# Tokens for the experts of a mixture-of-experts layer: indirect DMA and transposes in place of one-hot products

## The chip, the cores and the metric

The kernel runs on one core of one Trainium2 chip. The time is the device time of one launch in microseconds. A launch computes one layer of a decoder on 512 tokens: four mixers, then a mixture of experts. A core has a matrix engine (TensorE, PE in the profile; its weight loads stand apart as PEld), three engines for elementwise work (VectorE or DVE, ScalarE or ACT, GpSimd or POOL), SyncE (SP), whose instruction stream here only issues transfers, and 16 DMA engines that move the data. TensorE multiplies a stationary tile, loaded first, with a moving tile; its results go to PSUM banks.

## The reference

Only the second half bears on the change. Each of the 512 tokens (1024 columns) is normalized, the router takes the best 4 of 32 experts for it, and each expert is a gated two-layer network. The results are weighted with the gates and added to the token.

```python
h = rms_norm(x, norm2_g) * (1 + sc2) + sh2
logits = h @ router_w + router_b
top_vals, top_idx = lax.top_k(logits, 4)
gates = softmax(top_vals)
for e in range(32):                      # for the tokens that chose e
    hu = h[tokens] @ w_up[e] + b_up[e]   # 1024 -> 2048
    g, lin = min(hu[:, :1024], 7), clip(hu[:, 1024:], -7, 7)
    y = ((lin + 1) * g * sigmoid(1.702 * g)) @ w_down[e] + b_down[e]
    x[tokens] += gate2 * gates * y
```

All is float32. There are 2048 pairs of token and expert, 64 for an expert in the mean. The weights of the 32 experts are 12 MB each.

## The kernel before

**Two stages.** `emit_pre` (up to about 415 us) computes the modulation, the mixers, the output projection and the routing. The end of it routes the tokens in four tiles of 128: `route(tt)` normalizes a tile `a`, finds its experts, and `place` gives each token a position in each expert's list (`posm`). `emit_moe` (from 415 us on) runs the experts.

**Whole experts and pairs.** The experts are ranked by the number of their tokens. The 16 fullest are run one by one by `whole()`, with up to 128 slots for tokens each. In them each float32 factor is split into a rounded high part and the low rest, and three products replace one: high by high, high by low, low by high. So an expert's 24 weight tiles (8 for each half `hf` of the up projection, 8 for the down projection) are split too: ScalarE makes the high part (`high`, L1475), VectorE subtracts for the low one (`low`, L1480), and a step of six products follows on TensorE (L1610 to L1612 up, L1630 to L1632 down). The other 16 experts are run by `pairs()` two at a time, 64 slots each, in plain float32 products (L1678), each of the two on half of the columns of the array; no weights are split there.

**Order of the work.** `whole()` and `pairs()` are generators; the class `Tasks` takes pieces from both in turn by what each piece is worth (`PACE` is a step of a pair in units of a whole step), so a pair runs among steps of whole experts. TensorE, VectorE and ScalarE execute strictly in the order in which the program is written. The instructions of GpSimd and SyncE are put in order by the framework, and each engine then goes through its own list in that order.

**Weights.** Each weight tile of 1 MB comes by one DMA that SyncE issues (L1460 for the first expert, L1464 for the others) into a first-in-first-out list `fifo` of `RAW` = 8 buffers. A load waits until what read its buffer before is done: VectorE's split for a whole expert, TensorE's product for a pair.

**Tokens.** Before the experts run, all normalized tokens lie in SBUF as a high part `h2H` (ScalarE, L1207) and a low part `h2L` (VectorE, L1208). `select` writes a one-hot matrix (L252): column s of it has a one at the token that fills slot s. `gather_mm` (L261) multiplies `h2H` and `h2L` with it, so that the transposed tokens of two experts (or pairs) come out: 4 x 16 products with 256 columns in an event. `gather_end` (ScalarE, L269) scales and shifts them, and `gather_split` splits them. `slots` (L1490) multiplies the same one-hot matrix with a small table and gives each slot's gate and token number; it ran late in the expert, since only the end needs it. There are 8 such events in `whole()` and 4 in `pairs()`. The tokens of the first expert are built by `first()` while the tiles are routed.

**Bias and results.** A pair's up projection begins with its bias: a product (L1528) with a column `sc` that VectorE copies right before (L1701). An expert ends in `finish`: VectorE scales the result (L1522), and `add_rows` (L1502) adds it to the tokens in memory by an indirect DMA that GpSimd issues, 16 for the whole experts and 16 for the halves of the 8 pairs.

## Time and profile before

| | |
|---|---|
| time, median of 3 runs | 1570.74 us (1563.13 to 1571.32) |
| the profiled execution | 1570.13 us, span 1568.4 us |
| mean granted clock of TensorE | 0.956 of full speed |
| busy: TensorE | 1455.1 us, 93% of the span |
| busy: VectorE | 1018.1 us, 65% |
| busy: ScalarE | 720.2 us, 46% |
| busy: GpSimd | 231.0 us, 15% |
| moved by DMA | 469.54 MB, mean 299 GB/s |

The span is the time from the first to the last instruction that the profiler recorded; the execution's own time is a little longer. A busy share says how much of the span an engine was at work, not that it sets the end.

### The profile page before, as it was taken

The page shows a single profiled execution, that of the slowest core. Times are in us where ns is not written, and L with a number is a line of the kernel's source. Part 1 is how long each engine was busy: PE and PEld are TensorE (multiplying, and loading weights), DVE is VectorE, ACT ScalarE, POOL GpSimd, SP SyncE. Part 2 cuts the span into 40 slices and gives each one's busy share as a digit, 9 for nine tenths or more (in the row PEclk, how much of TensorE's full clock was granted, in tenths as well). Part 3 has the DMA queues.
Part 4 walks back from the last instruction along what each step waited for, and adds up shares of the span by engine and source line. Part 5 has one row for each costly group of instructions (what it writes and reads, how often), then busy time and mean ns, then how long its engine had stood idle before and what let it go on. Part 6 is the DMA issues. An engine that isn't in the chain of part 4 may idle for free.

```text
span 1568.4 us, 19785 instructions
## 1 busy us (share of the span) xinstructions
PE 1455.1 (93%) x6924; PEld 945.9 (60%) x6925; DVE 1018.1 (65%) x1607; ACT 720.2 (46%) x1036; POOL 231.0 (15%) x147
## 2 busy tenths in 40 slices
PE   6898998998979999999999999999999999899995
PEld 5676565666856565565655666565566656556553
DVE  7799776765765674666566565656666575666563
ACT  5463444653534454354544435444454444444441
POOL 3414154533310000000000000010010000001001
PEclk9998997999779999999999999999999999999998
DMA  8362432222647999889899988998999899799994
GB/s 346 111 228 95 135 121 68 88 84 88 235 176 297 375 407 397 306 342 404 347 385 420 403 345 313 393 367 350 421 400 371 331 387 407 308 406 399 398 396 124
DMA packets 73521, 469.54 MB, mean 299 GB/s; under 512 B 8532, under 2 KB 8932, under 8 KB 23240
## 3 DMA queue, kind: packets, MB, share of 16 engines
q1 hardware_dynamic: 70216, 457.21, 73.3%
q0 software_dynamic: 3200, 11.01, 3.7%
q8 instruction: 56, 0.92, 0.2%
q14 instruction: 49, 0.40, 0.1%
HBM read 454.55 MB, written 13.63 MB: 299 GB/s over the span
## 4 chain that ended last, share of the span: by engine, by line
issue 45%; DMA 12%; POOL 1%; POOLq 0%; DVE 0%
DMA out<-af,ii 12%; POOL out L1502 1%; POOLq L1502 0%; DVE af L1522 0%; DVE sc L1701 0%; POOLq L1806 0%
## 5 line engine op out<-in xcount | busy, mean ns | idle before, releaser
L1475 ACT CAST xr<-af 128x1024 fp32r<-128x1024 f32 x288 | 301.9, 1050 | 343.9 <-PE ps_w L1612 229.2
L1678 PE MATMUL ps_p<-af,xg 128*64 128x512 f32 x1536 | 364.1, 610 | 3.0 <-DMA af<-wexp 2.9
L1480 DVE TENSOR_TENSOR ar<-af,xr 128x1024 fp32r<-128x1024 f32 x192 | 235.6, 1230 | 121.3 <-PE ps_w L1611 55.6
L1678 PEld LDWEIGHTS ps_p<-af,xg 128*64 128x64 f32 x1536 | 109.8, 139 | 201.8 <-issue 190.9
L1502 POOL DMA_INDIRECT out<-af,ii x32 | 60.6, 1894 | 1058.5 <-DVE af L1522 919.2
L1610 PE MATMUL ps_w<-xr,ar 128*128 128x512 f32 x384 | 157.1, 409 | 0.0
L1480 DVE TENSOR_TENSOR xr<-af,xr 128x1024 fp32r<-128x1024 f32 x96 | 118.0, 1229 | 60.0 <-PE ps_w L1611 28.6
L1475 ACT CAST ar<-af 128x1024 fp32r<-128x1024 f32 x96 | 100.6, 1048 | 113.5 <-PE ps_w L1612 77.0
L1612 PE MATMUL ps_w<-xr,ar 128*128 128x512 f32 x384 | 151.5, 394 | 0.0
L1611 PE MATMUL ps_w<-ar,ar 128*128 128x512 f32 x320 | 126.7, 396 | 2.4 <-DVE ar L1480 2.4
L261 PEld LDWEIGHTS ps_m<-ar,xb 128*128 128x128 f32 x768 | 97.3, 191 | 18.2 <-issue 8.9
L1480 DVE TENSOR_TENSOR ar<-af,ar 128x1024 fp32r<-128x1024 f32 x64 | 78.2, 1221 | 44.4 <-issue 27.7
L261 PE MATMUL ps_m<-ar,xb 128*128 128x256 f32 (+1 forms) x768 | 100.9, 285 | 4.5 <-DVE ar L252 4.5
L1610 PEld LDWEIGHTS ps_w<-xr,ar 128*128 128x128 f32 x384 | 72.1, 188 | 40.3 <-issue 26.6
L1612 PEld LDWEIGHTS ps_w<-xr,ar 128*128 128x128 f32 x384 | 72.2, 188 | 16.9
L1630 PE MATMUL ps_w<-xr,ar 128*128 128x512 f32 x192 | 80.9, 421 | 0.0
L1611 PE MATMUL ps_w<-xr,ar 128*128 128x512 f32 x192 | 77.0, 401 | 1.2 <-DVE xr L1480 1.2
L1507 ACT ACTIVATE sb<-gb 128x512 f32<-128x512 f32 x48 | 30.4, 633 | 102.9 <-DVE gb L1506 102.9
L1631 PE MATMUL ps_w<-ar 128*128 128x512 f32 x192 | 76.4, 398 | 0.3 <-DVE ar L1480 0.2
L1632 PE MATMUL ps_w<-xr,ar 128*128 128x512 f32 x192 | 76.2, 397 | 0.0
L1611 PEld LDWEIGHTS ps_w<-ar,ar 128*128 128x128 f32 x320 | 60.4, 189 | 15.3 <-DVE ar L1480 4.4
L276 DVE TENSOR_TENSOR ar<-af,ar 128x512 fp32r<-128x512 f32 (+1 forms) x34 | 21.9, 645 | 58.7 <-ACT ar L275 58.5
(444 smaller groups left out, 2479.6 us busy)
## 6 DMA issues: line engine op xcount, KB each, us to landing
af<-wexp SPq DMA_DIRECT2D x384, 1024.0 KB, 9.4
af<-ada SPq DMA_DIRECT2D x32, 512.0 KB, 3.9
xa<-ada SPq DMA_DIRECT2D x4, 1024.0 KB, 11.3
af<-ada SPq DMA_DIRECT2D x4, 1024.0 KB, 15.5
xf<-wout SPq DMA_DIRECT2D x8, 512.0 KB, 3.7
xg<-wout SPq DMA_DIRECT2D x8, 512.0 KB, 3.6
out<-af SPq DMA_DIRECT2D x5, 512.0 KB, 3.0
af<-wG SPq DMA_DIRECT2D x6, 384.0 KB, 9.6
```

Of the source, the lines that this page charges most:

```text
L261: T.matmul(p[:, kk * 256:kk * 256 + n], h[:, tt, k * 128:(k + 1) * 128], Pm[:, tt, 0:n], start=kk == 0 and tt == 0 and h is h2H, stop=kk = ...
L1475: A.copy(wH[i % NH], w)
L1480: V.tensor_tensor(wL[i % NL], ahead.pop(0), wH[i % NH].bitcast(F32), op=OP.subtract)
L1502: G.indirect_dma_start(out=O, out_offset=bass.IndirectOffsetOnAxis(ap=idx, axis=0), in_=y, in_offset=None, compute_op=OP.add, bounds_check ...
L1507: act(sb, gb, AF.Sigmoid, scale=1.702)
L1610: T.matmul(b, xH[:, k, cs], H[:, s], start=k == 0, stop=False)
L1611: T.matmul(b, xH[:, k, cs], L[:, s], start=False, stop=False)
L1612: T.matmul(b, xL[:, k, cs], H[:, s], start=False, stop=False)
L1630: T.matmul(b, hTH[:, f], H[:, s], start=f == 0, stop=False)
L1631: T.matmul(b, hTH[:, f], L[:, s], start=False, stop=False)
L1632: T.matmul(b, hTL[:, f], H[:, s], start=False, stop=f == 7)
L1678: T.matmul(b[q * 64:q * 64 + 64], x(c % 8 + j)[:, q * 64:q * 64 + 64], w[:, j, s], skip_group_check=True, **kw(c % 8 + j))
```

## The change

The normalized tokens (`hn`) are stored to memory (`HN`) tile by tile as they are routed, from ScalarE's queue. The one-hot matrices stay, but only for the small product that gives gate and token number; that product and its selection now come before the gather, half an expert earlier. With the token numbers, GpSimd issues an indirect DMA (`gather_rows`, L256) that fetches the rows of an expert's or a pair's tokens from `HN` into `xgw` or `xgp`, one row for each of 128 slots; slots without a token keep what the buffer held. TensorE then transposes the rows (`gather_turn`, L264), 8 blocks for an expert or a pair. `h2H` and `h2L` are gone, and the space goes to two more weight buffers (`RAW` = 10) and to `xgw` and `xgp`. The copies `sc` for a pair's bias are written half an expert ahead (`bias_of`, L1705). The diff without the bookkeeping of the buffers' space:

```diff
--- before
+++ after
@@ gathering @@
-def gather_mm(T, p, k2, h2H, h2L, Pm, tts, n=256):
+def gather_rows(G, HN, x, idx):
+    G.indirect_dma_start(out=x, out_offset=None, in_=HN, in_offset=bass.IndirectOffsetOnAxis(ap=idx, axis=0), bounds_check=S - 1, oob_is_err=False)
+
+def gather_turn(T, p, k2, xs, ident):
     for kk in range(2):
         k = 2 * k2 + kk
-        for tt in tts:
-            for h in (h2H, h2L):
-                T.matmul(p[:, kk * 256:kk * 256 + n], h[:, tt, k * 128:(k + 1) * 128], Pm[:, tt, 0:n],
-                         start=kk == 0 and tt == 0 and h is h2H, stop=kk == 1 and tt == 3 and h is h2L, skip_group_check=True)
+        for j, x in enumerate(xs):
+            T.transpose(p[:, kk * 256 + j * 128:kk * 256 + j * 128 + 128], x[:, k * 128:(k + 1) * 128], ident)
@@ emit_pre: route(tt) @@
+                    act(hn, a, AF.Copy, scale=m2)
+                    A.dma_start(HN[tt * 128:(tt + 1) * 128], hn)
...
-                    act(h2["H"][:, tt], a, AF.Copy, scale=m2)
-                    i = V.scalar_tensor_tensor(h2["L"][:, tt], a, m2, h2["H"][:, tt].bitcast(F32), op0=OP.mult, op1=OP.subtract)
@@ emit_pre: first() @@
-                banks = [ps("acc") for _ in range(4)]
+                xg = res["xgw"] = M("xgw", [128, 2, D])
+                G.memset(xg, 0.0)
+                Pm, p = res["Pm"], ps("t")
                 for tt in range(4):
                     yield f"r{tt}"
-                    select(V, res["Pm"], iota, posm, [(0, 0, 128)], tt)
-                    for k2 in range(4):
-                        gather_mm(T, banks[k2], k2, res["h2H"], res["h2L"], res["Pm"], (tt,), 128)
+                    select(V, Pm, iota, posm, [(0, 0, 128)], tt)
+                    T.matmul(p[:, 0:4], Pm[:, tt], tok[:, tt], start=tt == 0, stop=tt == 3)
                     yield 1.0
+                _, idx = slots(V, t, tid, p)
+                gather_rows(G, HN, xg[:, 0], idx[0])
                 for k2 in range(4):
-                    gather_end(A, banks[k2], k2, xst[k2 % 2], cols, 128)
-                    gather_split(V.tensor_copy, G if OPT["gx"] >> k2 & 1 else V, k2, xst[k2 % 2], xH, xL, 128)
+                    p = ps("acc")
+                    gather_turn(T, p, k2, [xg[:, 0]], ident)
+                    gather_end(A, p, k2, xst[k2 % 2], cols, 128)
+                    gather_split(V.tensor_copy, V, k2, xst[k2 % 2], xH, xL, 128)
@@ emit_moe @@
-RAW = 8
+RAW = 10
...
+        xgp = M("xgp", [128, 2, D])
+        G.memset(xgp, 0.0)
@@ whole() @@
             def slots_of(r):
-                sl[r] = slots(lambda tt: Pm[:, tt, at(r):at(r) + 128], lambda tt: gx[:, tt, r])
+                for tt in range(4):
+                    select(V, Pm, iota, posr, [(r, 0, 128)], tt)
+                sl[r] = slot_mm(Pm, lambda tt: gx[:, tt, r])
+                if r:
+                    gather_rows(G, HN, xgw[:, r % 2], sl[r][1][0])
...
-                        if hf == 0 and k == 5 + 2 * (r == 0) and new:
-                            for tt in range(4):
-                                select(V, Pm, iota, posr, [(i, at(i), 128) for i in new], tt)
+                        if hf == (r == 0) and k in ((0, 1) if r == 0 else (3, 5)) and len(new) > k // 4 + (r == 0 and k):
+                            slots_of(new[k // 4 + (r == 0 and k)])
                         if hf and k == 2:
                             turn(0)
-                        if hf and k % 2 and new:
-                            gather(k // 2, 128 * len(new), later)
+                        if hf and k > 3 and new:
+                            gather(k - 4, new, later)
...
-                    if f in (4, 5) and len(new) > f - 4:
-                        slots_of(new[f - 4])
@@ pairs() @@
+            def slots_of(i):
+                r = NW + 1 + 2 * i
+                for tt in range(4):
+                    select(V, Pp, iota, posr, [(r + q, q * 64, 64) for q in range(2)], tt)
+                sl[i] = slot_mm(Pp, lambda tt: gx[:, tt, r:r + 2].rearrange("p r c -> p (r c)"), 2)
+                gather_rows(G, HN, xgp[:, i % 2], sl[i][1][0])
...
+            def bias_of(i, hf):
+                if i < PAIRS:
+                    sc, r = t("sc", [128, 128], F32R, bufs=2), NW + 1 + 2 * i
+                    V.tensor_copy(sc.rearrange("e (r s) -> e r s", s=64), bc(selc[:, hf, r:r + 2].bitcast(F32).unsqueeze(2), (128, 2, 64)))
+                    scs.append(sc)
...
                 if i == 0:
                     new = [n for n in (0, 1) if n < PAIRS]
-                    select_of(new)
-                    yield 0.5
+                    for n in new:
+                        slots_of(n)
+                        yield 0.5
+                    yield 2.0
...
-                    sc = t("sc", [128, 128], F32R, bufs=2)
-                    V.tensor_copy(sc.rearrange("e (r s) -> e r s", s=64), bc(selc[:, hf, r0:r0 + 2].bitcast(F32).unsqueeze(2), (128, 2, 64)))
                     banks = [ps("p", 2) for _ in range(2)]
-                    bias(banks, sc, True)
+                    bias(banks, scs.pop(0), True)
...
-                        if hf == 0 and k == 4 and new:
-                            select_of(new)
+                        if hf == 0 and k == 4:
+                            bias_of(i, 1)
+                        if hf == 0 and k in (2, 4) and len(new) > k // 2 - 1:
+                            slots_of(new[k // 2 - 1])
                         if hf and new:
-                            gather(k // 2, 128 * len(new))
+                            gather(k // 2, new)
...
-                    if f in (4, 6) and len(new) > f // 2 - 2:
-                        slots_of(new[f // 2 - 2])
+                    if f == 2:
+                        bias_of(i + 1, 0)
```

GpSimd's list before the change, its end: the 16 + 16 scatters of results (L1502) stand in one row after the last split (`ar` and `af` are slots of the two arenas of SBUF).

```order
L276 TENSOR_TENSOR ar_64<-af_62,ar_63 128x2x128 x2
L1439 TENSOR_TENSOR ar_64<-af_58,ar_64 32x1024 x2
L1245 TENSOR_TENSOR af_59<-af_59 128x512 x2
L1245 TENSOR_TENSOR af_58<-af_58,af_59 128x512 x2
L1502 DMA out<-af_58,ii 640x1024 x32
```

GpSimd's list after it, a part from the middle of the experts' stage: gathers for whole experts go into `xg_67`, those for pairs into `xg_66`; scatters (now L1518) come from `xa_68` (whole experts) and `af_60` (pairs, two in each).

```order
L1518 DMA out<-xa_68,ii 640x1024 x2
L256 DMA xg_67<-hn,ii 128x1024
L1518 DMA out<-af_60,ii 640x1024
L256 DMA xg_67<-hn,ii 128x1024
L1518 DMA out<-af_60,ii 640x1024
L1518 DMA out<-xa_68,ii 640x1024 x2
L256 DMA xg_67<-hn,ii 128x1024
L1518 DMA out<-af_60,ii 640x1024 x2
L256 DMA xg_67<-hn,ii 128x1024
L256 DMA xg_66<-hn,ii 128x1024 x2
```

Before, the list holds scatters alone from there on; now 23 gathers stand among them, some behind one or two scatters.

TensorE before the change, in an expert of rank 1 or above, one of the four parts of a gather event: 16 products (L261) stand between two steps of the expert's up projection.

```order
L1610 MATMUL ps_w<-xr_3043,ar_63 128x512
L1611 MATMUL ps_w<-ar_65,ar_63 128x512
L1612 MATMUL ps_w<-xr_3043,ar_64 128x512
L261 MATMUL ps_m<-ar_63,xb_2392 128x256
L261 MATMUL ps_m<-ar_63,xb_2393 128x256
...
L1610 MATMUL ps_w<-ar_64,ar_63 128x512
L1611 MATMUL ps_w<-xr_3043,ar_63 128x512
L1612 MATMUL ps_w<-ar_64 128x512
```

TensorE after it, such a part of the same kind of event (L1631 to L1633 are the expert's products now).

```order
L1631 MATMUL ps_w<-ar_64,ar_63 128x512
L1632 MATMUL ps_w<-xr_3000,ar_63 128x512
L1633 MATMUL ps_w<-ar_64 128x512
L264 MATMUL ps_m<-cst,xg_67 128x128 x4
L1631 MATMUL ps_w<-xr_3000,ar_63 128x512
L1632 MATMUL ps_w<-ar_65,ar_63 128x512
L1633 MATMUL ps_w<-xr_3000,ar_64 128x512
```

Four transposes of gathered rows stand where 16 products stood, and the parts lie one step apart (k = 4 to 7 of the second half) where they lay two apart.

VectorE before the change, where a pair's second half begins: the copy of the bias column (L1701) stands behind an activation and ahead of the weight splits (L1480).

```order
L1506 TENSOR_SCALAR gb<-ps_w 128x512
L1508 TENSOR_SCALAR af_60<-ps_w 128x512
L1509 SCALAR_TENSOR_TENSOR af_60<-af_60,gb 128x512
L1510 TENSOR_TENSOR af_60<-af_60,sb 128x512
L1701 CAST sc<-selc 128x128
L1480 TENSOR_TENSOR ar_65<-af_59,xr_3043 128x1024
```

VectorE after it, at the place that now holds a copy (L1705) for a later half; behind it stands the selection (L251) and the reading of the slots (L275, L276) that a gather waits for.

```order
L1525 SCALAR_TENSOR_TENSOR xa_68<-xa_68,gb 128x512
L1526 TENSOR_TENSOR xa_68<-xa_68,sb 128x512
L1504 TENSOR_TENSOR ar_65<-af_60,xr_3000 128x1024
L1504 TENSOR_TENSOR ar_65<-af_61,ar_64 128x1024
L1705 CAST sc<-selc 128x128
L251 TENSOR_SCALAR ar_63<-cst,posr 128x64 x8
L275 TENSOR_REDUCE gs<-ps_m 64x1
```

The copy has moved from right before the product that needs it to the middle of the half before.

## Rows read from the trace of the kernel before

**Rows 1.** The page's first section: busy us (share) xinstructions of each engine.

```profile
PE 1455.1 (93%) x6924; PEld 945.9 (60%) x6925; DVE 1018.1 (65%) x1607; ACT 720.2 (46%) x1036; POOL 231.0 (15%) x147
```

**Rows 2.** Windows: us, busy (xcount) of PE to POOL, granted clock, DMA share, GB/s.

```profile
415.00:467.00 52.00, 40.34 (x213) 31.26 (x214) 34.71 (x96) 21.81 (x33) 12.23 (x8) 0.83 0.56 213
467.00:1545.00 1078.00, 1037.69 (x4811) 650.03 (x4812) 667.29 (x890) 494.66 (x582) 56.36 (x29) 0.99 0.93 370
540.00:580.00 40.00, 40.00 (x178) 25.29 (x176) 27.05 (x29) 19.23 (x21) 2.29 (x1) 1.00 1.01 421
1100.00:1140.00 40.00, 40.00 (x174) 23.28 (x173) 27.11 (x29) 19.21 (x22) 0.00 (x0) 1.00 1.01 422
```

**Rows 3.** DMA, 467 to 1545: queues (packets, MB, share), then issues (KB, us to landing).

```profile
q1 hardware_dynamic: 53280, 388.00, 88.1%
q0 software_dynamic: 2928, 10.09, 4.7%
...
af<-wexp SPq DMA_DIRECT2D x370, 1024.0 KB, 9.7
out<-af,ii POOLq DMA_INDIRECT x29, 9.3
```

**Rows 4.** Waits of the loads' queue: waited for, us in total, times, longest.

```profile
SPq L1464 <- DVE ar L1480: 519.4, 115, 12.5
SPq L1464 <- DVE xr L1480: 238.1, 57, 11.1
```

**Rows 5.** Waits of TensorE, two rows, same columns.

```profile
PE ps_p L1528 <- DVE sc L1701: 24.9, 16, 2.5
...
PEld ps_p L1678 <- DMA af<-wexp: 6.3, 4, 2.8
```

**Rows 6.** Groups by line: busy us, mean ns | idle before them, what ended it.

```profile
L1678 PE MATMUL ps_p<-af,xg 128*64 128x512 f32 x1536 | 364.1, 610 | 3.0 <-DMA af<-wexp 2.9
...
L261 PE MATMUL ps_m<-ar,xb 128*128 128x256 f32 (+1 forms) x768 | 100.9, 285 | 4.5 <-DVE ar L252 4.5
...
L1515 PE MATMUL ps_m<-cst,af 128*128 128x128 f32 x128 | 19.4, 274 | 5.0 <-DVE af L1510 5.0
...
L1502 POOL DMA_INDIRECT out<-af,ii x32 | 60.6, 1894 | 1058.5 <-DVE af L1522 919.2 <-DMA out<-af,ii 75.2 <-DVE sc L1701 56.9
```

**Rows 7.** Timeline 409 to 416: start, us, engine, line, operation.

```profile
410.24 0.17 DVE L1259 TENSOR_SCALAR posm<-posm 128x32 f32<-128x32 f32 x1
410.32 1.28 DVE L1208 SCALAR_TENSOR_TENSOR xb<-af,ms,xb 128x1024 fp32r<-128x1024 f32 x1
...
411.94 3.65 PE L261 MATMUL ps_acc<-ar,xb 128*128 128x128 f32 x16 [0.34 <-DVE counts L1315]
...
415.39 0.73 PE L1610 MATMUL ps_w<-ar,ar 128*128 128x512 f32 x1
```

**Rows 8.** Timeline of TensorE, 445 to 468.

```profile
445.26 4.45 PE L261 MATMUL ps_m<-ar,xb 128*128 128x256 f32 x16 [4.55 <-DVE ar L252]
...
461.59 0.61 PE L1490 MATMUL ps_m<-gx,ar 128*128 128x8 f32 x4 [1.11 <-ACT xg L269]
463.53 0.58 PE L1490 MATMUL ps_m<-gx,ar 128*128 128x8 f32 x4 [1.33 <-DVE if L1497]
465.77 1.22 PE L1528 MATMUL ps_p<-ar,sc 128*128 128x512 f32 x2 [1.66 <-DVE sc L1701]
```

**Rows 9.** Timeline of GpSimd from 1140 us on.

```profile
1141.15 2.16 POOL L1502 DMA_INDIRECT out<-af,ii  x1 [57.89 <-DVE af L1522]
1151.63 1.51 POOL L1502 DMA_INDIRECT out<-af,ii  x1 [8.31 <-DMA out<-af,ii]
1159.74 2.30 POOL L1502 DMA_INDIRECT out<-af,ii  x1 [6.60 <-DMA out<-af,ii]
...
1555.51 1.41 POOL L1502 DMA_INDIRECT out<-af,ii  x1 [3.50 <-DMA out<-af,ii]
1561.01 1.44 POOL L1502 DMA_INDIRECT out<-af,ii  x1 [4.09 <-DMA out<-af,ii]
```

More of the change, by code (lines that the diff above doesn't have):

```diff
@@ L163, in __init__ @@
         self.peak = 0
-        self.own = n
+        self.short = set()
         self.oldest = False
@@ L169, in alloc @@
         for a, fr in enumerate(self.freed):
-            if a >= self.own and not short:
+            if a in self.short and not short:
                 continue
@@ L182, in alloc @@
                     size *= 2
-                cost = (a < self.own and short, nslots in (2, 4) and s % nslots > 0) + ((max(run), size) if self.oldest else (size, max(run)))
+                cost = (a not in self.short and short, nslots in (2, 4) and s % nslots > 0) + ((max(run), size) if self.oldest else (size, max(run)))
                 if best is None or cost < best[0]:
@@ L223, in extend @@
         ar.freed += [[0] * 8 for _ in range(n)]
-        if stay:
-            ar.own = len(ar.tiles)
+        if not stay:
+            ar.short |= set(range(len(ar.tiles) - n, len(ar.tiles)))
     def shrink(self, n, dt):
@@ L230, in shrink @@
         del ar.tiles[-n:], ar.freed[-n:]
-        ar.own = min(ar.own, len(ar.tiles))
     def __call__(self, key, shape, dt=F32):
@@ L1480, in low, with slot_mm @@
                 V.tensor_tensor(wL[i % NL], ahead.pop(0), wH[i % NH].bitcast(F32), op=OP.subtract)
[L1482 removed]
+        Pm, xH, xL, xgw = (res[n] for n in ("Pm", "xH", "xL", "xgw"))
         hTH = M("hTH", [128, 8, 128], F32R)
         hTL = M("hTL", [128, 8, 128], F32R)
[L1486 removed]
+        def slot_mm(Px, gx_of, nc_=1):
             p = ps("m", 2)
             for tt in range(4):
[L1490 to L1499 removed]
+                T.matmul(p[:, 0:4 * nc_], Px[:, tt], gx_of(tt), start=tt == 0, stop=tt == 3)
+            return slots(V, t, tid, p, nc_)
         def add_rows(y, idx):
@@ L1538, in slots_of, with gather @@
             def slots_of(r):
-                sl[r] = slots(lambda tt: Pm[:, tt, at(r):at(r) + 128], lambda tt: gx[:, tt, r])
-            def gather(k2, n, later):
-                p = ps("m", 2)
-                gather_mm(T, p, k2, h2H, h2L, Pm, range(4), n)
+                for tt in range(4):
[3 more added lines that the diff above has]
+                    gather_rows(G, HN, xgw[:, r % 2], sl[r][1][0])
+            def gather(k2, new, later):
+                p, n = ps("m", 2), 128 * len(new)
+                gather_turn(T, p, k2, [xgw[:, i % 2] for i in new], ident)
                 def end():
@@ L1646, in pairs, with gather @@
             Pp = res["Pp"]
-            def select_of(new):
+            def slots_of(i):
+                r = NW + 1 + 2 * i
                 for tt in range(4):
-                    select(V, Pp, iota, posr, [(NW + 1 + 2 * i + q, i % 2 * 128 + q * 64, 64) for i in new for q in range(2)], tt)
-            def slots_of(i):
-                c, r = i % 2 * 128, NW + 1 + 2 * i
-                sl[i] = slots(lambda tt: Pp[:, tt, c:c + 128], lambda tt: gx[:, tt, r:r + 2].rearrange("p r c -> p (r c)"), 2)
+                    select(V, Pp, iota, posr, [(r + q, q * 64, 64) for q in range(2)], tt)
+                sl[i] = slot_mm(Pp, lambda tt: gx[:, tt, r:r + 2].rearrange("p r c -> p (r c)"), 2)
+                gather_rows(G, HN, xgp[:, i % 2], sl[i][1][0])
             later = []
-            def gather(k2, n):
-                p = ps("m", 2)
-                gather_mm(T, p, k2, h2H, h2L, Pp, range(4), n)
+            def gather(k2, new):
+                p, n = ps("m", 2), 128 * len(new)
+                gather_turn(T, p, k2, [xgp[:, i % 2] for i in new], ident)
                 later.append(lambda: gather_end(A, p, k2, xt[:, 2 * k2:2 * k2 + 2], cols, n))
@@ L1738, in overflow @@
             xs = raw[0][:, 0].rearrange("p (a b) -> p a b", a=8)
+            g_, idx = slot_mm(Pf, lambda tt: gxr[:, 4 * tt:4 * tt + 4])
+            rows = raw[1][:, 1]
+            gather_rows(G, HN, rows, idx[0])
             for k in range(8):
                 p = ps("m", 2)
-                for i, (h, tt) in enumerate([(h, tt) for tt in range(4) for h in (h2H, h2L)]):
-                    T.matmul(p[:, 0:128], h[:, tt, k * 128:(k + 1) * 128], Pf[:, tt], start=i == 0, stop=i == 7)
+                T.transpose(p[:, 0:128], rows[:, k * 128:(k + 1) * 128], ident)
                 V.tensor_scalar(xs[:, k], p[:, 0:128], cols["sc2"][:, k:k + 1], cols["sh2"][:, k:k + 1], op0=OP.mult, op1=OP.add)
-            g_, idx = slots(lambda tt: Pf[:, tt], lambda tt: gxr[:, 4 * tt:4 * tt + 4])
             hT = raw[0][:, 1].rearrange("p (a b) -> p a b", a=8)
```

89 lines of the change are left out of this document (41 added, 48 removed).

## Prediction

> **What bounds the kernel now.** I read four views of the stage in which the experts run, from 415 us to the end. First the busy times: TensorE is busy 1455.1 of 1568.4 us [rows 1], and in the 1078 us from the first pair of experts to the last loads (467 to 1545) 1037.7 us, at a granted clock of 0.99 [rows 2]. Then who waits for whom: TensorE waits for expert weights in four places, 6.3 us in all [rows 5], and its pair products stood idle 3.0 us [rows 6]. So weights come in time, and TensorE sets the end. The third view is the one that a reader would skip after that: the DMA engines are nearly full as well. In the same 1078 us their share is 0.93; in 40-us stretches without a gather of tokens it is 1.01, at 421 to 422 GB/s, and it does not go higher [rows 2]. Loads take 88.1% for 388.0 MB and the scatters of results 4.7% for 10.09 MB [rows 3]. Fourth, why the share isn't 1: the queue that issues the loads waits 519.4 + 238.1 us for a buffer that VectorE has yet to split [rows 4]; TensorE holds the buffers back. Two limits lie close together, TensorE first and DMA some 7% behind. An edit that frees TensorE is worth what it frees only until the DMA engines are full.
>
> **The change part by part.**
>
> *Products removed.* The gather by one-hot products is the 768 matmuls of L261 into ps_m: 100.9 us, 0.131 us each, with 4.5 us of waiting for the one-hot columns [rows 6]. All lie on TensorE's path. The 64 products that build the first expert's tokens before the stage are counted in "start of the stage" below.
>
> *Transposes added.* 15 whole experts and 8 pairs give 23 blocks of 8 transposes: 184. The same operation stands at L1515: 128 take 19.4 us, 0.152 us each [rows 6]. So +28 us.
>
> *The bias column moved.* The bias product of a pair waits 24.9 us in 16 places for a small VectorE copy (sc) that is queued behind weight splits [rows 5]. The copy is now written half an expert earlier, as the order of VectorE shows. Where it moves, it costs VectorE what it cost before; behind it wait only splits, which have three steps of slack. I take -24.9 us.
>
> *Selections* keep their number and size, so VectorE's work is unchanged in the experts' stage.
>
> *Start of the stage.* Before, the last position is known at 410.41, VectorE forms a low part for 1.28 us, and the products of 3.65 us run from 411.94; the first expert product starts at 415.39 [rows 7]. Now the low part is gone (-1.28), 8 transposes (1.2 us, twice that at half clock) stand for the 3.65 us (-1.9), but three things are added in a row: a slot product (0.6 us, [rows 8]), four small VectorE operations such as the one of 0.17 us [rows 7] (0.7 us), and an indirect DMA. The trace has no gather; the nearest thing is a scatter, where GpSimd could start the next one 5.5 us after it began one, in the quiet end of the kernel (1555.51 to 1561.01), and 8.1 us and 10.5 us later in the full stage [rows 9]. I take 5.5 us here. Sum +4 us; between +1 (a gather lands in 2 us, less than any row) and +9 (10.5 us).
>
> *Start of the pairs.* 80 of the 768 products stand here. With the waits of 4.55, 1.11, 1.33 and 1.66 us that precede the pair's parts [rows 8], 10.5 + 8.6 us go. In their place come 20 transposes (3 us) and a wait for the rows: two gathers in a queue (2 x 1.9 us on GpSimd, [rows 6], then 8.1 us, and 0.7 us of VectorE ahead: 12.6 us) against some 6.5 us of TensorE work between slot product and transpose in the new order. Wait 6 us. Net -10 us.
>
> *Sum by TensorE alone:* 1568.4 - 100.9 - 4.5 - 2.4 (the waits of 1.11 and 1.33) - 24.9 + 28 + 4 + 6 = 1474 us span.
>
> *What the DMA engines then need.* In the 1078 us they are full for 0.93, 1002.5 us. Added: 19 of the 24 gathers fall in it, 128 rows of 4 KB or 0.524 MB each, 10 MB. At the loads' price (0.881 x 1078 us for 388.0 MB: 2.45 us a MB) that is 25 us, at the scatters' (0.047 x 1078 us for 10.09 MB: 5.0 us a MB) 50 us [rows 3]. A scatter adds to memory and so reads and writes it; a gather only reads, like a load. I take 25. Two more weight buffers let 2 MB come before the stretch: -5 us. That makes 1022 us at a share of 1.00, 56 us less than 1078; at 1.01, 66 us less; with dear gathers, 30 us less. TensorE's own 990 us or so would fit into it. So the buffers, not TensorE, run dry, and what TensorE gains beyond 56 us comes back as waits for weights.
>
> The row for this limit is the flat 421 to 422 GB/s. The Trainium skill (DMA: Bandwidth & Descriptors, Specifications) puts the fabric's ceiling at 435 GB/s and one core's share of memory at about 358 GB/s. By the first the 408 MB would take 939 us and TensorE would stay the bound; by the second they would take 1140 us and the change could give nothing. The trace lies above the second already and 3% below the first, and decides.
>
> *Stores of the normalized rows* (four of 0.5 MB, issued from ScalarE) and the memsets of the new tiles lie in the stage before, hidden by the routing chain of the last tokens; if that cover is gone the first gather waits for the last store, some 3 us, within the +9 above. The low parts that VectorE no longer forms (three more of 1.28 us) were hidden behind ScalarE and TensorE, except the last.
>
> **Sum.** 1568.4 + 4 - 10 - 56 = 1506 us span. The profiled execution took 1570.13, 1.7 us beyond its span; the median shown is 1570.74. So 1508; I put 1510, as the share cannot be 1.00 in the last steps.
>
> **Rivals.**
>
> *A, TensorE still sets the end: 1474 + 1.7 = 1476 us.* This needs the loads to run faster than now when TensorE takes buffers faster, or the gathers to be nearly free. For it: ten buffers in place of eight. Against it: with eight the flat stretches already reach 1.01, and 97% of the time they would need is taken by bytes that stay.
>
> *B, the gathers come late: slower.* All indirect DMAs leave one queue, GpSimd's, in program order; a scatter there waits for the scatter before it, since both add to the same memory. The new order puts gathers behind such scatters: twice behind one of a pair's two, twice behind both. A gather behind two scatters starts 10.5 + 8.1 us late and needs 8 to 10 itself: 27 to 29 us, against some 19 us of TensorE work (about 80 products of 364.1/1536 = 0.237 us, [rows 6], by the order of the instructions) from the last slot product to the first transpose. TensorE takes work strictly in order, so a late transpose stops the experts too, and the clock with it: where it idled at 440 to 467, the granted clock was 0.83 for that stretch [rows 2]. Only four of the twelve events can be hit by that, for 8 to 10 us, or 36 us, about TensorE's slack under the DMA limit. The end comes out slower than now by 0.5% (1578 us) when all twelve events lose 8 us or more, that is when a gather takes 27 us from its slot product on the average: 1510 + 12 x 8.7 - 36 = 1578. For it: scatters do wait so, 10.5 and 8.1 us. Against it: 1.9 us on GpSimd and 9.3 us to land [rows 6, 3] make about 13 us for an undelayed gather.
>
> The Trainium skill (SBUF — State Buffer, SBUF: two separate sides) warns that descriptors which GpSimd writes are held up while VectorE holds the port that the two share, and gives 3.1 us in place of 0.6 for one such DMA. Here a scatter's issue takes 1.9 us beside a VectorE that is busy 62% of the time and 1.4 us at the quiet end [rows 6, 9]: half a microsecond, which would not make B true.
>
> *C, the DMA engines need more than I count:* dear gathers (+25) and a start that waits 10.5 us per gather (+10): 1545 us.
>
> **How the numbers follow.** My forecast, the DMA engines full: 0.72, with 1490 to 1546 as its own range (the 1.01 share and a quick start at one end, C at the other). A: 0.09. B in its mild form, up to 1563: 0.06; B just undoing the gain: 0.05; B slower: 0.08. About 0.5%, 8 us, is what a measurement here can tell from no change. So faster 0.87, same 0.05, slower 0.08. The range of 8 in 10 runs from halfway to A, 1484, to 1548.
>
> **What would show it.** In the changed profile: between the first pair and the last loads the DMA share near 1.00 and some 400 GB/s; TensorE and the casts of ScalarE waiting for wexp loads, tens of microseconds where there were 6.3; TensorE's busy time lower by about 75 us; the queue's waits for VectorE's splits gone down; no wait of L1528's like for sc; gathers landing in 6 to 10 us. Wrong would be: a DMA share that stays near 0.93 with TensorE waiting for xgw or xgp (B), or TensorE without waits and a span near 1474 (A).

## The result, and the profile after

The changed kernel takes 1502.05 us (median of 4 runs, 1496.42 to 1505.14) against 1569.11 us before: a ratio of 0.9574, 95% interval 0.9534 to 0.9614. Forecast were 1510 us, within 1484 to 1548. The profiled execution took 1502.2 us with a span of 1500.5 us.

The page's first section after the change, to be read beside [rows 1]:

```profile
PE 1382.2 (92%) x6288; PEld 869.9 (58%) x6289; DVE 1017.6 (68%) x1616; ACT 714.4 (48%) x1036; POOL 272.0 (18%) x171
```

TensorE lost 72.9 us of busy time and the span 67.9 us, so its share looks the same. The windows tell more; columns as in [rows 2]. The first is the start of the experts' stage, the second the stretch from there to 1480 us, called the long stretch below (the last load lands by 1472 us; before, by 1539 us of the 1545):

```profile
410.00:470.00 60.00, 36.87 (x168) 27.02 (x169) 41.13 (x118) 20.22 (x30) 18.29 (x11) 0.77 0.61 227
467.00:1480.00 1013.00, 981.91 (x4302) 592.28 (x4300) 667.38 (x884) 495.34 (x593) 88.11 (x49) 0.99 0.99 399
540.00:580.00 40.00, 38.12 (x168) 22.57 (x168) 27.87 (x36) 18.61 (x20) 2.85 (x2) 1.00 1.02 406
1000.00:1040.00 40.00, 39.75 (x182) 23.64 (x180) 27.73 (x32) 24.44 (x32) 1.44 (x1) 1.00 1.02 413
```

The DMA share of the long stretch rose from 0.93 to 0.99, and 40-us stretches with gathers and scatters in them stand at 1.02 now. The queues and issues of 467 to 1480 us, beside [rows 3]:

```profile
q1 hardware_dynamic: 53054, 386.28, 92.0%
q0 software_dynamic: 5952, 17.32, 6.9%
...
af<-wexp SPq DMA_DIRECT2D x331, 1024.0 KB, 15.7
xa<-wexp SPq DMA_DIRECT2D x37, 1024.0 KB, 15.5
xg<-hn,ii POOLq DMA_INDIRECT x20, 9.1
```

A load takes 15.7 us from issue to landing where it took 9.7: with ten buffers more loads are under way at once and share engines that are full (12.1 us with eight buffers in e3_raw8, further down). The waits for weights grew, but look small (all engines' waits, columns as in [rows 5]):

```profile
PE ps_m L1514 <- DVE ar L251: 16.8, 13, 3.0
...
PEld ps_p L1696 <- DMA af<-wexp: 15.3, 13, 3.2
...
PE ps_p L1696 <- DMA af<-wexp: 7.1, 6, 2.3
```

So TensorE is busy 0.97 of the long stretch and the DMA engines 0.99. From the profile alone either could be called the bound; the experiments below had to tell. The queue of the loads waits 446.5 + 207.3 us for VectorE's splits, down from 757.5 us in [rows 4]. No row for a wait of the bias product (L1544) for `sc` is left. The new operations, by line:

```profile
L1696 PE MATMUL ps_p<-af,xg 128*64 128x512 f32 x1384 | 364.2, 604 | 7.1 <-DMA af<-wexp 7.1
...
L264 PE MATMUL ps_m<-cst,xg 128*128 128x128 f32 x184 | 29.0, 277 | 2.0 <-ACT xg L288 1.1 <-DMA xg<-hn,ii 0.7
...
L264 PE MATMUL ps_acc<-cst,xg 128*128 128x128 f32 x8 | 1.9, 424 | 7.7 <-DMA xg<-hn,ii 7.7
```

The 184 transposes take 29.0 us (28 forecast), and behind the first expert they wait 0.7 us for gathered rows in the whole stage (their weight loads 1.5 us). Only the first expert's rows are waited for at length, 7.7 us. The start in the timeline, beside [rows 7], from the last position to the first product of an expert:

```profile
408.62 0.17 DVE L1279 TENSOR_SCALAR posm<-posm 128x32 f32<-128x32 f32 x1
...
412.03 1.20 POOL L256 DMA_INDIRECT xg<-hn,ii  x1 [13.64 <-DMA af<-wexp]
...
419.01 1.94 PE L264 MATMUL ps_acc<-cst,xg 128*128 128x128 f32 x8 [7.72 <-DMA xg<-hn,ii]
...
421.18 0.80 PE L1631 MATMUL ps_w<-ar,ar 128*128 128x512 f32 x1 [0.23 <-DVE ar L294]
```

The gather takes 7.0 us from GpSimd's start to the first transpose. Then TensorE from 438 us to the first pair, beside [rows 8]:

```profile
438.96 0.77 PE L1514 MATMUL ps_m<-gx,ar 128*128 128x4 f32 x4 [2.73 <-DVE ar L251]
...
450.50 1.35 PE L1514 MATMUL ps_m<-gx,ar 128*128 128x8 f32 x4 [2.94 <-DVE ar L251]
453.72 1.03 PE L1514 MATMUL ps_m<-gx,ar 128*128 128x8 f32 x3 [1.86 <-DVE ar L251]
...
461.11 0.77 PE L1514 MATMUL ps_m<-gx,ar 128*128 128x4 f32 x4 [3.01 <-DVE ar L251]
...
474.56 0.64 PE L1696 MATMUL ps_p<-af,xg 128*64 128x512 f32 x1
```

Four slot products wait 10.5 us here for the selections right ahead of them. The first pair starts at 474.56 us; before it was 466.92. The change lost 7.6 us up to there, and gained 75.6 us behind: from the first pair to the end it takes 1025.9 us, where it took 1568.4 - 466.92 = 1101.5. I call this the main stretch; it serves as a second measure below, since the start of the first expert's product lies anywhere from 414.4 to 425.5 us in the profiled executions of the changed kernel and its variants.

### The profile page after: what moved, and what is told of

The parts are those of the page before. It is cut to its first block, busy times and chain, and to the rows that moved or that the text cites. A ratio compares the mean times of both kernels' runs of the same rounds, so it can differ in the third digit from the quotient of the medians.

```text
span 1500.5 us, 18591 instructions
## 1 busy us (share of the span) xinstructions
PE 1382.2 (92%) x6288; PEld 869.9 (58%) x6289; DVE 1017.6 (68%) x1616; ACT 714.4 (48%) x1036; POOL 272.0 (18%) x171
## 3 DMA queue, kind: packets, MB, share of 16 engines
q0 software_dynamic: 6656, 19.41, 5.3%
## 5 line engine op out<-in xcount | busy, mean ns | idle before, releaser
L1499 ACT CAST xr<-af 128x1024 fp32r<-128x1024 f32 x249 | 260.4, 1048 | 258.0 <-PE ps_w L1633 160.3
L1696 PE MATMUL ps_p<-af,xg 128*64 128x512 f32 x1384 | 364.2, 604 | 7.1 <-DMA af<-wexp 7.1
L1504 DVE TENSOR_TENSOR ar<-af,xr 128x1024 fp32r<-128x1024 f32 x165 | 203.0, 1232 | 105.4 <-PE ps_w L1632 48.1
L1518 POOL DMA_INDIRECT out<-xa,ii x16 | 33.6, 2100 | 722.5 <-DVE xa L1538 722.5
L1631 PE MATMUL ps_w<-xr,ar 128*128 128x512 f32 x384 | 160.7, 418 | 0.0
L1633 PE MATMUL ps_w<-xr,ar 128*128 128x512 f32 x384 | 151.4, 394 | 0.0
L1504 DVE TENSOR_TENSOR xr<-af,xr 128x1024 fp32r<-128x1024 f32 x84 | 103.3, 1230 | 48.7 <-issue 26.8
L1632 PE MATMUL ps_w<-ar,ar 128*128 128x512 f32 x320 | 127.2, 398 | 1.1 <-DVE ar L1504 1.0
L1504 DVE TENSOR_TENSOR ar<-af,ar 128x1024 fp32r<-128x1024 f32 x64 | 78.2, 1221 | 30.4 <-PE ps_w L1632 15.7
L1631 PEld LDWEIGHTS ps_w<-xr,ar 128*128 128x128 f32 x384 | 72.4, 189 | 40.5 <-issue 24.7
L1633 PEld LDWEIGHTS ps_w<-xr,ar 128*128 128x128 f32 x384 | 72.5, 189 | 17.4
L1632 PE MATMUL ps_w<-xr,ar 128*128 128x512 f32 x192 | 77.1, 401 | 1.0 <-DVE xr L1504 1.0
L1696 PE MATMUL ps_p<-xa,xg 128*64 128x512 f32 x152 | 69.5, 599 | 0.0
L1632 PEld LDWEIGHTS ps_w<-ar,ar 128*128 128x128 f32 x320 | 60.6, 189 | 14.2 <-DVE ar L1504 3.4
L256 POOL DMA_INDIRECT xg<-hn,ii x24 | 35.3, 1472 | 150.4 <-DVE ii L280 53.6
L1499 ACT CAST xr<-xa 128x1024 fp32r<-128x1024 f32 x39 | 40.8, 1046 | 39.4 <-PE ps_w L1633 25.8
```

Source lines behind the costliest of these rows:

```text
L256: G.indirect_dma_start(out=x, out_offset=None, in_=HN, in_offset=bass.IndirectOffsetOnAxis(ap=idx, axis=0), bounds_check=S - 1, oob_is_err ...
L1499: A.copy(wH[i % NH], w)
L1504: V.tensor_tensor(wL[i % NL], ahead.pop(0), wH[i % NH].bitcast(F32), op=OP.subtract)
L1518: G.indirect_dma_start(out=O, out_offset=bass.IndirectOffsetOnAxis(ap=idx, axis=0), in_=y, in_offset=None, compute_op=OP.add, bounds_check ...
L1631: T.matmul(b, xH[:, k, cs], H[:, s], start=k == 0, stop=False)
L1632: T.matmul(b, xH[:, k, cs], L[:, s], start=False, stop=False)
```

## The experiments

All results, with the main stretch (span less the start of the first pair's product) of the profiled execution. The kernel before ran beside each group, at 1564.6 to 1568.9 us.

| run | median us | ratio to before, 95% | first pair at | main stretch |
|---|---|---|---|---|
| before | 1569.1 | | 466.9 | 1101.5 |
| changed kernel | 1502.1 | 0.9574 (0.9534 to 0.9614) | 474.6 | 1025.9 |
| e1_less_dma | 1485.1 | 0.9482 (0.9440 to 0.9524) | 474.9 | 1009.3 |
| e2_less_pe | 1502.8 | 0.9587 (0.9551 to 0.9622) | 482.2 | 1023.8 |
| e10_less_both | 1455.1 | 0.9281 (0.9233 to 0.9329) | 475.4 | 978.4 |
| e5_less_dma_before | 1557.6 | 0.9935 (0.9914 to 0.9956) | 461.3 | 1090.6 |
| e4_before_bias | 1545.8 | 0.9870 (0.9835 to 0.9906) | 466.5 | 1076.5 |
| e3_raw8 | 1515.5 | 0.9692 (0.9653 to 0.9731) | 472.7 | 1038.9 |
| e6_tiny_gather | 1482.2 | 0.9473 (0.9429 to 0.9518) | 469.7 | 1009.3 |
| e7_skip_empty | 1500.0 | 0.9551 (0.9521 to 0.9580) | 480.7 | 1024.5 |
| e9_tiny_scatter | 1477.4 | 0.9439 (0.9406 to 0.9471) | 471.4 | 999.9 |
| e8_ahead | 1508.3 | 0.9630 (0.9591 to 0.9669) | 481.8 | 1025.6 |
| v1_pool_select | 1498.0 | 0.9574 (0.9543 to 0.9605) | 471.9 | 1029.0 |
| v2_pace192 | 1502.5 | 0.9600 (0.9570 to 0.9630) | 474.1 | 1025.7 |

### Who sets the pace: fewer loads, fewer products, both

My theory D: the DMA engines, full, set the pace of the main stretch. The rival T: TensorE, busy for 0.97 of it, still does. One run takes work from the one, one from the other.

```diff
-                ws = [load(r, c // 2) for r in rs]
+                ws = [load(rs[0], c // 2)]
+                ws.append(ws[0] if c // 2 % 4 == 3 else load(rs[1], c // 2))
```

> The changed kernel, but in one of four steps of a pair both experts use the first one's weights, so 24 of 384 loads of 1 MB (6%) fall away while TensorE's work stays (the results of the pairs are then wrong by that). Theory D, the DMA engines (share 0.99 between first pair and last loads) set the pace now: their need falls from about 1000 to 940 us, TensorE takes over, and the time falls by what TensorE's slack was, some 13 to 25 us: 1477 to 1489 us, with a DMA share near 0.95. Rival T, TensorE still sets the end and the full DMA engines are a coincidence: 1502 us, within 4 us.

```diff
-                            T.matmul(b, xL[:, k, cs], H[:, s], start=False, stop=False)
+                            if k % 4 != 1:
+                                T.matmul(b, xL[:, k, cs], H[:, s], start=False, stop=False)
...
-                        T.matmul(b, hTL[:, f], H[:, s], start=False, stop=f == 7)
+                        if f % 4 != 1:
+                            T.matmul(b, hTL[:, f], H[:, s], start=False, stop=f == 7)
```

> The changed kernel without the third product (low tokens by high weights) in one of four steps of the whole experts: 192 products of 0.237 us or 45 us less TensorE work, all loads and splits kept (the results lose accuracy). Theory D: only the start of the stage, where the DMA engines aren't full, gains: 1494 to 1502 us, and the freed time turns up as TensorE's waits for weights or their splits. Rival T: 45 us less, 1457 us.

Fewer loads gave 17 us, in the middle of what D expected; 45 us less work for TensorE gave nothing (1502.8 us, main stretch 2 us shorter). So T doesn't hold for the changed kernel. The long stretch of the two, e1_less_dma first, then e2_less_pe:

```profile
467.00:1480.00 1013.00, 972.79 (x4312) 580.95 (x4312) 669.50 (x886) 495.21 (x593) 90.59 (x52) 0.99 0.95 375
```

```profile
467.00:1480.00 1013.00, 965.42 (x4115) 571.90 (x4117) 670.22 (x899) 491.78 (x594) 90.37 (x50) 0.98 0.99 400
```

Without the 24 loads the DMA share falls to 0.95, as expected, but a part of that is the window: the last load of e1_less_dma has landed by 1450 us. From 475 to 1455 us the changed kernel and e1_less_dma, in this order, show 1.00 and 0.97:

```profile
475.00:1455.00 980.00, 950.22 (x4156) 572.30 (x4154) 650.16 (x865) 479.21 (x572) 87.19 (x48) 0.99 1.00 404
```

```profile
475.00:1455.00 980.00, 954.54 (x4230) 570.90 (x4230) 660.94 (x877) 487.30 (x581) 86.17 (x48) 0.99 0.97 385
```

No row of a wait for weights is left at TensorE in e1_less_dma. In e2_less_pe the share stays at 0.99, and TensorE, with some 43 us of products less in this stretch (180 of 0.237 us), shows only 16 us less of busy time. Where the rest went stands in two more rows of e2_less_pe, the group of the pairs' products and the wait of their weight loads:

```profile
L1698 PE MATMUL ps_p<-af,xg 128*64 128x512 f32 x1384 | 381.0, 606 | 13.9 <-DMA af<-wexp 13.9
```

```profile
PEld ps_p L1698 <- DMA af<-wexp: 35.4, 32, 3.4
```

The same 1384 products have 381.0 us of busy time where they had 364.2, and the waits for weights at their weight loads went from 15.3 to 35.4 us. The mean of one product is 606 ns where it was 604, so the products weren't slower: they start further apart, and as the record of one lasts 0.6 us while the next follows 0.43 us after it (475.04 and 475.47 us in the first pair), a short wait between them leaves no gap. Part of the waiting counts as busy. All 1536 products of the pairs together (the row above leaves out those with weights in `xa`) are busy 365.7 us in the changed kernel and 386.1 us in e2_less_pe, but 352.6 us in e1_less_dma, where none waits for weights. So a busy share of 0.97 was no proof that TensorE was the bound.

The third run has both edits.

> Both edits, e1_less_dma (24 loads less) and e2_less_pe (45 us of products less), in one kernel; alone the first gave -17 us and the second nothing. If the floor at 1485 us that e1_less_dma and e6_tiny_gather reached is TensorE's, the second edit now pays: 1440 to 1460 us. Rival: the floor is another one (VectorE's and ScalarE's splits, the waits inside a pair): 1475 to 1485 us.

The second edit, worth nothing alone, is worth 30 us behind the first (1485.1 to 1455.1). So the floor at 1485 us was TensorE's. Its long stretch, up to 1430 us:

```profile
467.00:1430.00 963.00, 925.60 (x4104) 544.32 (x4103) 664.55 (x882) 489.83 (x593) 87.21 (x49) 0.99 0.98 394
```

Not all of the 45 us came. The DMA engines are nearly full again, at 0.98, but TensorE shows no wait for weights here either. Its busy time over the whole span falls by 36.9 us against e1_less_dma (1368.1 to 1331.2), and its waits for VectorE, ScalarE and gathered rows grow from 25 to 36 us (476 to 1425 us). Whether the DMA engines have a part in what is missing isn't shown.

The same loads taken from the kernel before:

> The kernel before with the edit of e1_less_dma: 24 of 384 loads fall away, TensorE's work stays (the pairs' results are wrong by that). Theory D, in which TensorE set the end before and DMA came some 7% behind: no change but the 6 us of weight waits, 1560 to 1568 us. Rival: weights bounded the kernel before as well, in a way that the waits don't show: 1550 us or less, as the changed kernel gained 17 us by the same edit.

It gained 11 us where I had expected 6 or less, so the loads already cost the kernel before a little; but the 17 us of the changed kernel are more, and before most of the 24 loads went unnoticed (62 us of DMA time at 2.45 us a MB). Some of these 11 us were hidden in busy time as well: the 1536 products of the pairs are busy 364.1 us before and 359.2 us in this run, which has no row of waits for weights at TensorE.

### The parts of the change

The bias copies alone, in the kernel before (`bias_of` is the change's function):

```diff
-                    sc = t("sc", [128, 128], F32R, bufs=2)
-                    V.tensor_copy(sc.rearrange("e (r s) -> e r s", s=64), bc(selc[:, hf, r0:r0 + 2].bitcast(F32).unsqueeze(2), (128, 2, 64)))
...
-                    bias(banks, sc, True)
+                    bias(banks, scs.pop(0), True)
...
+                        if hf == 0 and k == 4:
+                            bias_of(i, 1)
...
+                    if f == 2:
+                        bias_of(i + 1, 0)
```

> The kernel before, with only the copies of the pairs' bias columns written half an expert ahead. If TensorE set the end before, as the prediction has it, the 24.9 us that TensorE waited for the copies go: 1569 less 25 or 1544 us, DMA share up from 0.93 to 0.95. Rival: the DMA engines were so near their limit that other waits take their place: 1555 us or more.

The main stretch is 25.0 us shorter, where [rows 5] has 24.9 us (so close a match of two single executions is partly luck), and the median 21.6 us. A wait on the bound engine was worth its length as long as the DMA engines had room (share 0.94 from 467 to 1525 us).

The two weight buffers:

```diff
-RAW = 10
+RAW = 8
```

> The changed kernel with 8 weight buffers in place of 10. By the prediction the two buffers are worth the 2 MB that come before the full stretch, 5 us: 1507 us, DMA share still 0.98 or more. Rival: the two buffers are what lifts the DMA share from 0.93 to 0.99, as loads now wait less for a buffer: with 8 the share falls back to 0.95 or 0.96 and the time rises to 1525 to 1545 us.

Between the two: 13.5 us, where the prediction had 5 and the rival 20 or more. The two buffers do two things. They bring 2.0 MB ahead of the stretch: the loads' queue moves 386.88 MB behind the first pair in e3_raw8 (472.7 to 1490 us) and 384.87 MB in the changed kernel (474.56 to 1480 us). That is 4.8 us at 2.41 us a MB, the prediction's figure. And they keep the DMA engines a little fuller. From 480 to 1450 us the changed kernel, e2_less_pe, e8_ahead and the two v runs, all with ten buffers, move 403 or 404 GB/s, this one 399; from 475 to 1455 us, to be read beside the changed kernel's row above:

```profile
475.00:1455.00 980.00, 946.76 (x4100) 569.04 (x4098) 640.68 (x854) 472.40 (x561) 86.56 (x48) 0.99 0.99 399
```

One per cent of some 1000 us is 10 us. So the rival was right in kind, with a share that falls from 1.00 to 0.99 and not to 0.95. The two parts add up to 15 us, a little more than the 13.5 measured.

### What gathers and scatters cost full DMA engines

```diff
-                    gather_rows(G, HN, xgw[:, r % 2], sl[r][1][0])
+                    gather_rows(G, HN, xgw[0:4, r % 2], sl[r][1][0][0:4])
...
-                gather_rows(G, HN, xgp[:, i % 2], sl[i][1][0])
+                gather_rows(G, HN, xgp[0:4, i % 2], sl[i][1][0][0:4])
```

> The changed kernel, but each gather in the experts' stage (23 of 24) fetches 4 rows in place of 128 (the other slots keep zeros, so the results are wrong); its place in GpSimd's queue and the transposes stay. Theory D: the gathers' bytes, 6.6 MB in the full stretch at a share of 0.068 - 0.047, some 21 to 25 us of the DMA engines, come back as time until TensorE sets the end, as with the missing loads: 1482 to 1489 us. Rival: gathers cost by their count and latency, not by their rows, or TensorE sets the end: 1500 us.

19.8 us less, as D has it. So it is the gathers' bytes that cost; their number and order are unchanged here, and TensorE's waits for weights fall to 3.0 us all the same. The row of the gathers' and scatters' queue (467 to 1455 us) has 5.3% of 988 us, 52 us, where it was 6.9% of 1013 us, 70 us:

```profile
q0 software_dynamic: 3536, 10.41, 5.3%
```

The next run tried to make something of it for the kernel itself.

```diff
-                                 compute_op=OP.add, bounds_check=S + 127, oob_is_err=True)
+                                 compute_op=OP.add, bounds_check=S - 1, oob_is_err=False)
```

> The changed kernel, but a scatter skips slots without a token (bound at 511 in place of 639) where it added them to 128 spare rows of memory. The scatters go through 4 x 128 + 12 x 96 + 16 x 64 = 2688 slots for 2048 pairs of token and expert, so 24% of their share of 0.047 x 1078 = 50 us, 12 us, would be freed. Theory D: 1490 us. Rivals: TensorE sets the end, or a skipped row costs the DMA engines what a written one does: 1502 us.

A miss: 1500.0 us, main stretch 1.4 us shorter, TensorE's waits for weights the same (15.4 and 7.0 us); no difference that could be told. To see whether scatters cost anything at all, the next run left nearly all of their rows out:

```diff
-                add_rows(y[q * n:q * n + n], ix[0:n])
+                add_rows(y[q * n:q * n + 4], ix[0:4])
```

> The changed kernel, but each scatter adds only the first 4 rows of its 64 to 128 (the rest of the results is left out), its place in GpSimd's queue stays. It is to tell why the skipping of empty slots bought nothing. If every byte that leaves the full DMA engines is worth its time, some 9.7 MB at 405 GB/s or 24 us by bytes, 45 us by their share go, more than the 17 us that e1_less_dma found: 1481 to 1486 us, 2 us of it in the tail. Rival: a scatter, unlike a load or a gather, runs beside the loads without delaying them, or only where buffers are full anyway: 1497 to 1502 us.

25 us less: scatters do delay the loads. No wait for weights is left at TensorE, and the 1536 products of the pairs are busy 352.5 us, as in e1_less_dma, so this is TensorE's floor again. The main stretch is 9.4 us below that of e1_less_dma. The three quicker scatters at the end give 3.8 us of it: from TensorE's last product to the end it takes 12.8 us, where e1_less_dma takes 16.6. Waits for gathered rows that e1_less_dma has and this run hasn't are another 3.2 us; the rest I can't place. The queue's row in both (467 to 1480 us of e7_skip_empty, 467 to 1450 us of e9_tiny_scatter):

```profile
q0 software_dynamic: 5961, 15.10, 5.8%
```

```profile
q0 software_dynamic: 3736, 7.08, 2.1%
```

Skipping empty slots keeps the packets (5961, as 5952 in the changed kernel) and takes 2.2 MB of 17.3 away. By bytes that is 5.4 us at 2.41 us a MB, by share 11 us; 1.4 to 2 us were seen. The intervals of the two ratios leave room for the 5 us, hardly for the 11. Why the share's figure didn't come stays open.

### Three attempts at a faster version

The start of the stage, where the DMA engines are at 0.61, should pay for any time that TensorE gains there. Selections one step ahead of their slot products (the whole experts' part; the pairs' part is alike):

```diff
+            def select_of(r):
+                for tt in range(4):
+                    select(V, Pm, iota, posr, [(r, 0, 128)], tt)
...
+                        if at_ in (0, gap) and len(new) > at_ // gap:
+                            slots_of(new[at_ // gap])
+                        if at_ in (-1, gap - 1) and len(new) > (at_ + 1) // gap:
+                            select_of(new[(at_ + 1) // gap])
```

> The changed kernel with each selection written one step of TensorE ahead of its slot product, where it stands right before it. TensorE's waits for the selection are 16.8 us, 10.6 of them in four places between 436 and 464 us, ahead of the full stretch. If these waits cost their length there, and DMA sets the pace behind them: 1492 to 1497 us. Rival: VectorE, busy 8 to 9 tenths from 430 to 460 us with splits and selections, is the limit there, and the waits only move: 1500 to 1504 us.

6 us more at the median, though the intervals just overlap; nothing was gained, as the rival had it. From the first expert's product to the first pair it took 57.0 us in place of 53.4. The waits moved, and one of them to a gather: the second pair's now starts 40.8 us after the first expert's product, where it was 35.6 (TensorE in e8_ahead):

```profile
454.73 1.35 PE L1514 MATMUL ps_m<-gx,ar 128*128 128x8 f32 x4 [3.66 <-DVE ar L251]
...
472.73 0.90 PE L264 MATMUL ps_m<-cst,xg 128*128 128x128 f32 x3 [4.18 <-DMA xg<-hn,ii]
```

The same selections on GpSimd:

```diff
-                    select(V, Pm, iota, posr, [(r, 0, 128)], tt)
+                    select(G if r < 3 else V, Pm, iota, posr, [(r, 0, 128)], tt)
...
-                    select(V, Pp, iota, posr, [(r + q, q * 64, 64) for q in range(2)], tt)
+                    select(G if i < 2 else V, Pp, iota, posr, [(r + q, q * 64, 64) for q in range(2)], tt)
```

> The changed kernel, but the selections of the first two pairs and of ranks 0 to 2 (28 small operations, 6 us of VectorE between 438 and 465 us) run on GpSimd. In the stretch of the first expert VectorE is busy 8 to 9 tenths, TensorE 5 to 8, and the DMA engines 0.6. Theory: VectorE, by splits and selections in one queue, holds the start up; then the first pair comes 4 to 6 us earlier, and as the full DMA stretch behind it keeps its length, the time falls as much: 1496 to 1499 us. Rival: GpSimd is slower at them and has the bias stores in its queue: 1502 us or more, with TensorE waiting for GpSimd in VectorE's place.

The median lies in the range of the theory, but the kernel before was 4.5 us quicker beside this run as well, and the ratio is that of the changed kernel, 0.9574: no gain that can be measured. From the first expert's product to the first pair it took 52.2 us in place of 53.4, not the 4 to 6 us less that I had expected. And the tail:

```diff
-PACE = 1.96
+PACE = 1.92
```

> The changed kernel with a pace of 1.92 in place of 1.96, so that the last pair ends 7 steps of the last whole expert (10 us) before the end, where the last expert and the last pair ended together and three scatters went out one after the other (1481.6, 1487.5 and 1492.5 us, end 1500.5). If only the tail changes, one scatter is left behind TensorE's last product: 5 to 6 us less, 1496 us. Rival: the pairs draw their weights earlier from DMA engines that are full already, and TensorE waits for them: 1502 us or more.

No gain. The pair's two scatters went out earlier, but the last expert ended later by about what was won, its scatter behind theirs (GpSimd's timeline in v2_pace192; in the changed kernel they began at 1481.59, 1487.54 and 1492.51):

```profile
1478.52 2.15 POOL L1518 DMA_INDIRECT out<-af,ii  x1 [42.61 <-DVE af L1538]
...
1484.34 2.02 POOL L1518 DMA_INDIRECT out<-af,ii  x1 [3.68 <-DMA out<-af,ii]
...
1491.38 1.43 POOL L1518 DMA_INDIRECT out<-xa,ii  x1 [5.02 <-DMA out<-af,ii]
```

None of the versions beats the changed kernel.

## Why the prediction was right

**The mechanism.** The step that decided it, that TensorE's gain is worth something only until the DMA engines are full, held, and e1_less_dma, e2_less_pe and e10_less_both show it. Rival A, TensorE alone, had 1476 us; the floor that appears when loads, gathers or scatters are taken away lies at 1477 to 1485 us. So the kernel stands some 17 to 25 us above what TensorE alone would allow. One reading under it was too simple: that weights came in time before, as TensorE waited 6.3 us for them. Taking loads away gained 11 us there (e5_less_dma_before), part of it waiting that the profile counts as busy.

**The terms.** The sum had 1568.4 + 4 - 10 - 56 = 1506 us of span; measured is 1500.5. That it is so near is partly luck, as terms that were off cancel, the start by +14 and the full stretch by -17. (The range's lower end of 1484 us is halfway to A from 1490, the low end of the forecast's own range, not from 1510.)

- *Start of the stage*, +4: the first expert product came 5.8 us later than before. The gather took 7.0 us where I took 5.5 from the scatters.
- *Start of the pairs*, -10: it came out at +1.9 (53.4 us from the first expert's product to the first pair's, where it was 51.5), though 4.2 us of that are three more steps of the first expert done by then (13 of 1.4 us, where it was 10). This is the step that failed. I had let the waits of [rows 8] go and put a wait of 6 us for the rows in their place. The rows weren't waited for. The selections were: each slot product now has its own right ahead of it on VectorE's list, and the four waits of 10.5 us stand where four waits of 8.65 us stood, 4.55 us of them for a selection.
- *The full stretch*, -56, from 1078 to 1022 us between the first pair and the last loads: it took 1005 us (474.6 to 1480), at the share that was forecast (0.99 to 1.00). Two prices were too high. Gathers: 19 us (6.9% of 1013 us less 4.7% of 1078 us), not 25, since a slot without a token fetches nothing: over the whole run the 24 gathers moved 19.41 - 11.01 = 8.40 MB, 2048 rows of 4 KB, or 0.35 MB each in place of 0.524. Loads: 0.920 x 1013 us for 386.28 MB is 2.41 us a MB, not 2.45, which over 386 MB is 13 us (why the price fell isn't shown). Both windows end 6 to 8 us behind the last load; what follows them is 3 us shorter, 20.5 us for 23.4.
- *The weight buffers*, -5 within that: 13.5 us by e3_raw8. The 2 MB came as forecast. That the buffers also keep the DMA engines fuller, 403 to 404 GB/s for 399, the sum had at nothing.
- *Products, transposes and bias copies* were right: 100.9 + 4.5 us are gone, 29.0 us came, and the 24.9 us are 21.6 by the median of e4_before_bias, 25.0 by its main stretch.

**What would show it.** I had asked for tens of microseconds of waits for weights. The rows show 15.3 and 7.1 us at TensorE and 13.0 us at ScalarE's casts; the rest is inside the products' busy time, as e2_less_pe showed. Gathers landed in 9.1 us (6 to 10 forecast), and TensorE's busy time fell by 72.9 us (75).

**Rival B**, late gathers: the transposes waited 0.7 us in all for rows after the first expert. The places where a gather stands behind scatters exist, and had slack enough. In e10_less_both, which takes work from TensorE, the mechanism can be seen: a gather that GpSimd starts at 1335.17 us, behind two scatters, keeps TensorE waiting for 4.09 us. Rival C's dear gathers didn't come either.

The Trainium skill's rule (SBUF — State Buffer, SBUF: two separate sides), by which VectorE holds up the descriptors that GpSimd writes, to 3.1 us for one DMA, doesn't show in these traces: the 24 gathers took 1.47 us each on GpSimd in the mean, 1.03 to 2.10 us, beside a VectorE busy two thirds of the time, the one at the start of the stage 1.20 us. What the spread comes from isn't shown.

## What to carry to other kernels

When an edit frees the bound engine, work out what the second one will need for the time that would be left, at the price per byte of the rows, with every transfer that the edit adds; the smaller of the two gains is the forecast. To tell two engines at 0.97 and 0.99 apart, take work from each alone and then from both: the bound is the one whose work counts alone. And follow a wait that seems to go with the operation it stood before: if what it waited for stays on the same list, the wait comes back at the next operation that needs it.

## What was unexpected of the hardware

- *A busy TensorE that waits.* The 1536 products of the pairs are busy 352.5 us where no weights are waited for (e9_tiny_scatter), 365.7 us in the changed kernel and 386.1 us where TensorE has less else to do (e2_less_pe): up to 34 us of waiting that counts as busy.
- *DMA engines have no sharp top in the share.* It reads up to 1.02, at 406 to 413 GB/s with gathers and scatters in the stretch, and 1.01 at 421 to 422 GB/s without [rows 2].
- *The clock in the patchy start.* TensorE's granted clock of 10-us windows in the changed kernel, ahead of the first pair:

```profile
440.00:450.00 10.00, 5.25 (x30) 3.06 (x28) 8.33 (x12) 3.70 (x5) 5.74 (x4) 0.91 0.48 182
450.00:460.00 10.00, 5.52 (x14) 4.04 (x14) 8.66 (x36) 1.32 (x2) 3.34 (x3) 0.58 0.88 322
...
470.00:480.00 10.00, 9.80 (x50) 5.55 (x49) 4.13 (x5) 6.58 (x13) 0.00 (x0) 1.00 0.69 233
```

While it was busy for half of the time it fell to 0.58, which is mostly its lower level of 1.2 GHz, and it was back at 1.00 when the products stood close again. A product of the first expert (L1632) took 0.63 us there and 0.39 to 0.40 us before and after, so if it is the small waits of the start that lower the clock, which no run here isolates, they cost more than their own length.
